# Low parts of weight tiles made by an accumulating DMA in a two-layer hybrid decoder kernel

## The chip, the cores and the metric

The kernel runs on one core of a Trainium2 chip. The metric is the device time of one execution in microseconds (us); lower is better. TensorE is called PE in the rows, its weight loads PEld, VectorE DVE, ScalarE ACT, GpSimd POOL, SyncE SP.

## What is computed

One inference step of a two-layer decoder trunk on 576 token rows (a prompt of 512 and 8 samples of 8), width 1024. All matrix products are in float32. The core of it is

```python
def swiglu(x, w_gate, w_up, w_down):
    return (jax.nn.silu(x @ w_gate) * (x @ w_up)) @ w_down
# each layer
x = x + 0.5 * swiglu(rms_norm(x, ffn1_norm), ffn1_w_gate, ffn1_w_up, ffn1_w_down)    # inner width 2816
proj = rms_norm(x, mix_norm) @ w_in                                                   # 1024 x 3092
...                                    # pool, GLA, HGRN2 and SSD mixers on parts of proj
x = x + jnp.concatenate([o_pool, o_gla, o_hgrn, o_ssm], axis=-1) @ w_out
x = x + 0.5 * swiglu(rms_norm(x, ffn2_norm), ffn2_w_gate, ffn2_w_up, ffn2_w_down)
```

with a last `rms_norm` after the two layers and new mixer states as further outputs.

## The kernel before

Every float32 product is made of three products of rounded operands. A weight tile w (128 rows, up to 1024 columns, that is up to eight 128x128 blocks) is split by `two_parts` into hi, w rounded to float32r, and lo = w - hi; activations are split alike by `split`. `gemm` then runs hi·hi (line 256), lo·hi (line 257) and hi·lo (line 258) for each block, in this order, so a tile's lo is wanted one matmul after its hi.

The host lays all weight tiles one after another into `wts` and lists them in `PLAN`, one entry (`what`, `at`, `n`, `tail`) per use, 491 in all, in the order in which PE takes them. `what` 0 is a tile used as it lies in memory. The feed-forward stages also multiply by a scheme with 7 products in place of 8: a round (`glu7`) takes four tiles b11, b21, b22, b12 from memory and makes seven operands of them in `ORDER` 1, 5, 6, 7, 3, 2, 4. Operand 1 is b11 itself, 2 is b12 and 4 is b22; 5, 6, 7 and 3 are sums and differences that VectorE makes in the `raws` buffers. There are 39 such rounds. A group of a feed-forward stage is up to three rounds and then eight tiles of the down projection (256 to 768 columns). Between the two feed-forward stages of a layer stands the mixer, whose 32 projection and output tiles without tail are all `what` 0, interleaved by `interleave` with the recurrences' small operations on every engine.

`weight()` hands the next tile to the matmuls and first prepares the tile three further on (`LOOKAHEAD` 3): `load` issues the DMA from `wts` on SP's queue into `raw` (2 buffers) or `raws` (4 buffers, shared with sums), and `two_parts` writes `whi` and `wlo` (4 buffers each). The buffers of the tile three ahead are those of the tile before the one just started, so a split can't begin before PE has read that one to its end. In the trace this shows as ACT waiting for line 258 ahead of line 195. The three last tiles of a stage that ends in a norm are marked `tail` and live in another pool. Within an engine instructions run in the order that the framework's scheduler gave them; nothing is reordered on the chip.

POOL has little to do: squares at the start, small copies in the mixers, and the shifted sums of the pooling mixer (`pool`, line 1197). It issues no DMA.

Of the kernel before, what the change touches and what calls it, by code (L numbers as in the profile page):

```python
# [5 lines left out]
F32 = mybir.dt.float32  # L6
F32R = mybir.dt.float32r
# [3 lines left out]
AF = mybir.ActivationFunctionType  # L11
ALU = mybir.AluOpType
# [95 lines left out]
class Trunk:  # L108
# [77 lines left out]
        return acts, self.sums(acts, self.first_norm(), range(KD))  # L186


    def two_parts(self, src, n, tail=False):
        nc = self.nc  # L190
        size = n if tail else 1024
        pool, th, tl, bufs = self.tail if tail else (self.wp, "whi", "wlo", (4, 4))
        hi = pool.tile([P, size], F32R, name="whi", tag=th, bufs=bufs[0])
        lo = pool.tile([P, size], F32R, name="wlo", tag=tl, bufs=bufs[1])
        nc.scalar.copy(hi[:, :n], src[:, :n])  # L195
        nc.vector.tensor_tensor(lo[:, :n], src[:, :n], hi[:, :n].bitcast(F32), ALU.subtract)  # L196
        return hi, lo

    def load(self, i, n, pool, tag, bufs):
# [4 lines left out]
    def prep(self, i):  # L204
        what, at, n, tail = self.plan[i]
        if what == 0:
            self.w[i] = self.two_parts(self.load(at, n, self.wp, "raw", 2), n, tail)
            return

        tt = self.nc.vector.tensor_tensor  # L210
        if what == 1:
            self.blocks = {11: self.load(at, n, self.sp, "raws", 4)}
            src = self.blocks[11]
        b = self.blocks
        if what == 5:
            b[21] = self.load(at + 1, n, self.sp, "raws", 4)
            b[22] = self.load(at + 2, n, self.wp, "raw", 2)
            b[12] = self.load(at + 3, n, self.wp, "raw", 2)
            src = b[0] = self.sp.tile([P, 1024], F32, name="raws", tag="raws", bufs=4)
            tt(src, b[21], b[22], ALU.add)  # L220
        elif what == 6:
            src = b[11]
            tt(b[21], b[11], b[21], ALU.subtract)
            tt(src, b[0], b[11], ALU.subtract)
        elif what == 7:
            src = b[21]
        elif what == 3:
            src = b[0]
            tt(src, b[12], b[11], ALU.subtract)
        elif what == 2:  # L230
            src = b[12]
        elif what == 4:
            src = b[22]
        self.w[i] = self.two_parts(src, n)

    def weight(self):
        i = self.wi
# [1294 lines left out]
```

## Time and profile before

| | |
|---|---|
| median of 3 runs | 2303.1 us (2296.84 to 2305.1) |
| the profiled execution | 2301.83 us, its span 2300.0 us |
| granted TensorE clock, mean | 0.989 of 2.4 GHz |
| busy: PE, DVE, ACT, POOL | 98%, 70%, 44%, 2% |
| read from memory | 180.36 MB, 81 GB/s over the span |
| share of the 16 DMA engines taken by SP's queue | 25.4% |

PE is busy in nearly all of the span, so a time saved elsewhere counts only where PE stands still or runs at the lower clock, and a time added counts where it makes PE wait. Matmul durations in the rows overlap: the starts of successive matmuls lie 0.13 us apart for 288 columns while each is listed with 0.29 us.

### The profile page before, as it was taken

The numbers are of one execution on the slowest core, as the hardware profiler recorded it, in microseconds if no ns is written. First come the engines' busy times: TensorE is split into PE (matmuls) and PEld (weight loads), VectorE is DVE, ScalarE is ACT, GpSimd is POOL, SyncE is SP. The second block draws the span as 40 slices with busy tenths as digits, with TensorE's granted clock in tenths as the row PEclk, the third lists the DMA queues.
The fourth block names the chain that finished last, engine by engine and source line by source line (L and its number), as shares of the span: only waits on it lengthen the run. The fifth ranks groups of instructions, "written<-read, shape, count | busy, mean of one in ns | idle before, by whom it ended". The sixth has DMA issues, their size and how long they took to land.

```text
span 2300.0 us, 40667 instructions
## 1 busy us (share of the span) xinstructions
PE 2253.3 (98%) x16721; PEld 2168.6 (94%) x16721; DVE 1619.4 (70%) x3049; ACT 1010.7 (44%) x1844; POOL 45.6 (2%) x94
## 2 busy tenths in 40 slices
PE   7999999999999999999999999999999999999997
PEld 6999999987978999999999999999889899999997
DVE  7775767777567876666697666767775688767575
ACT  3452534634424534344454443446344435435352
POOL 1000000000010000000000000000000100000000
PEclk9999999999989999999999999999999899999998
DMA  4232223211212133232313323232112131332322
GB/s 153 73 105 86 94 81 101 80 47 60 76 42 89 55 101 95 81 111 74 119 42 97 106 85 95 65 122 63 44 51 76 52 113 47 101 92 83 92 76 76
DMA packets 63146, 189.91 MB, mean 83 GB/s; under 512 B 7120, under 2 KB 13552, under 8 KB 62448
## 3 DMA queue, kind: packets, MB, share of 16 engines
q1 hardware_dynamic: 62816, 187.31, 25.4%
q8 instruction: 131, 2.15, 0.4%
q14 instruction: 55, 0.45, 0.1%
q10 hardware_dynamic: 144, 0.00, 0.0%
HBM read 180.36 MB, written 6.93 MB: 81 GB/s over the span
## 4 chain that ended last, share of the span: by engine, by line
PE 88%; DVE 7%; ACT 3%; DMA 1%; issue 1%; POOL 0%; ACTq 0%; DVEq 0%; SPq 0%
PE mm L258 21%; PE mm L256 21%; PE mm L257 20%; PE lv L256 3%; PE lv L258 3%; PE lv L257 3%; PE ms L258 2%; PE ms L257 2%; PE ms L256 2%; DVE wlo L196 1%; ACT whi L195 1%; PE lv L1182 1%; DMA raw<-wts 1%; DVE att L1187 1%; PE ms L1157 1%
## 5 line engine op out<-in xcount | busy, mean ns | idle before, releaser
L256 PE MATMUL mm<-h,whi 128*128 128x288 f32 (+2 forms) x1872 | 563.1, 302 | 10.0 <-ACT h L127 6.9
L258 PE MATMUL mm<-h,whi 128*128 128x288 f32 (+2 forms) x1872 | 558.6, 301 | 4.3 <-DVE h L128 4.2
L257 PE MATMUL mm<-h,wlo 128*128 128x288 f32 (+2 forms) x1872 | 560.0, 300 | 0.6 <-DVE wlo L196 0.6
L196 DVE TENSOR_TENSOR wlo<-raw,whi 128x1024 fp32r<-128x1024 f32 (+2 forms) x296 | 314.7, 1065 | 226.4 <-ACT whi L195 224.5
L256 PE MATMUL mm<-a,whi 128*128 128x256 f32 (+2 forms) x1408 | 414.5, 295 | 1.4 <-ACT a L278 1.3
L258 PE MATMUL mm<-a,whi 128*128 128x256 f32 (+2 forms) x1408 | 414.1, 295 | 0.6
L257 PE MATMUL mm<-a,wlo 128*128 128x256 f32 (+2 forms) x1408 | 414.3, 294 | 0.0
L256 PEld LDWEIGHTS mm<-h,whi 128*128 128x128 f32 x1872 | 357.6, 191 | 24.1 <-issue 10.6
L195 ACT CAST whi<-raw 128x1024 fp32r<-128x1024 f32 (+2 forms) x296 | 272.0, 921 | 242.7 <-PE mm L258 205.7
L258 PEld LDWEIGHTS mm<-h,whi 128*128 128x128 f32 x1872 | 356.6, 191 | 10.0 <-DVE h L128 5.5
L257 PEld LDWEIGHTS mm<-h,wlo 128*128 128x128 f32 x1872 | 357.5, 191 | 2.9 <-issue 1.6
L195 ACT CAST whi<-raws 128x1024 fp32r<-128x1024 f32 x195 | 204.7, 1050 | 178.2 <-PE mm L258 156.1
L196 DVE TENSOR_TENSOR wlo<-raws,whi 128x1024 fp32r<-128x1024 f32 x195 | 238.2, 1222 | 55.2 <-ACT whi L195 54.9
L258 PEld LDWEIGHTS mm<-a,whi 128*128 128x128 f32 x1408 | 263.8, 188 | 4.2 <-DVE a L279 4.1
L256 PEld LDWEIGHTS mm<-a,whi 128*128 128x128 f32 x1408 | 264.7, 188 | 2.1 <-ACT a L278 2.1
L257 PEld LDWEIGHTS mm<-a,wlo 128*128 128x128 f32 x1408 | 264.6, 188 | 0.0
L430 DVE SCALAR_TENSOR_TENSOR x<-mm,x 128x320 f32<-128x320 f32 (+2 forms) x256 | 116.6, 456 | 160.7 <-PE mm L258 160.2
L256 PE MATMUL mm<-more,whi 128*128 128x288 f32 x624 | 184.8, 296 | 0.4 <-ACT u L488 0.4
L257 PE MATMUL mm<-more,wlo 128*128 128x288 f32 x624 | 184.8, 296 | 0.3 <-DVE wlo L196 0.3
L258 PE MATMUL mm<-more,whi 128*128 128x288 f32 x624 | 185.0, 297 | 0.0
L256 PEld LDWEIGHTS mm<-more,whi 128*128 128x128 f32 x624 | 117.3, 188 | 1.5 <-ACT more L278 0.8
L257 PEld LDWEIGHTS mm<-more,wlo 128*128 128x128 f32 x624 | 117.5, 188 | 0.5 <-DVE wlo L196 0.5
(334 smaller groups left out, 3894.8 us busy)
## 6 DMA issues: line engine op xcount, KB each, us to landing
raw<-wts SPq DMA_DIRECT2D x156, 512.0 KB, 3.6
raw<-wts SPq DMA_DIRECT2D x106, 384.0 KB, 3.0
raws<-wts SPq DMA_DIRECT2D x78, 512.0 KB, 4.2
raw<-wts SPq DMA_DIRECT2D x32, 256.0 KB, 2.6
x<-x SPq DMA_DIRECT2D x4, 576.0 KB, 5.3
Ss<-sssm SPq DMA_DIRECT2D x2, 1024.0 KB, 6.0
nssm_s<-Ss SPq DMA_DIRECT2D x2, 1024.0 KB, 4.1
y<-x SPq DMA_DIRECT2D x4, 320.0 KB, 2.4
```

The source lines that it names most:

```text
L195: nc.scalar.copy(hi[:, :n], src[:, :n])
L196: nc.vector.tensor_tensor(lo[:, :n], src[:, :n], hi[:, :n].bitcast(F32), ALU.subtract)
L256: mm(ps[:, :n], wh, ah, start=(first and i == 0), stop=False)
L257: mm(ps[:, :n], wl, ah, start=False, stop=False)
L258: mm(ps[:, :n], wh, al, start=False, stop=(final and i == last))
L430: self.nc.vector.scalar_tensor_tensor(x, pd[:, :n], 0.5, x, ALU.mult, ALU.add)
L1157: nc.tensor.matmul(pu[d * s:d * s + d, :], kw[64:, si, d * s:d * s + d], vm[64:].rearrange("p b d -> p (b d)"), start=True, stop=True)
L1182: nc.tensor.matmul(lv[r, 0:4 * half], kc[:, 0], g2, start=True, stop=True)
L1187: nc.vector.copy_predicated(a2, mask.to_broadcast([n, 8, nb, w]), lv[r, 0:8 * half].rearrange("p (s b w) -> p s b w", s=8, w=w))
```

## The change

`two_parts` gets the tile's place in `wts` for 305 of the 491 operands: for `what` 0 without tail from the plan's thirteenth entry on, and for operands 1, 2 and 4 of the rounds. By width these are 181 of 1024 columns, 94 of 768, 28 of 512 and 2 of 256, together 139.5 MB; 117 of the 181 are those of the rounds. For them ScalarE writes -w, rounded to float32r, into `wlo`; POOL issues a DMA that reads the tile from memory once more and adds it onto `wlo`; then ScalarE writes `whi`. VectorE's subtraction falls away. The other 186 operands are made as before.

```diff
-    def two_parts(self, src, n, tail=False):
+    def two_parts(self, src, n, tail=False, at=None):
...
-        nc.scalar.copy(hi[:, :n], src[:, :n])
-        nc.vector.tensor_tensor(lo[:, :n], src[:, :n], hi[:, :n].bitcast(F32), ALU.subtract)
+        if at is None:
+            nc.scalar.copy(hi[:, :n], src[:, :n])
+            nc.vector.tensor_tensor(lo[:, :n], src[:, :n], hi[:, :n].bitcast(F32), ALU.subtract)
+        else:
+            nc.scalar.activation(lo[:, :n], src[:, :n], AF.Copy, scale=-1.0)
+            nc.gpsimd.dma_start(lo[:, :n], self.I["wts"][at, :, :n].bitcast(F32R), accum_op=ALU.add)
+            nc.scalar.copy(hi[:, :n], src[:, :n])
         return hi, lo
...
         if what == 0:
-            self.w[i] = self.two_parts(self.load(at, n, self.wp, "raw", 2), n, tail)
+            raw = self.load(at, n, self.wp, "raw", 2)
+            self.w[i] = self.two_parts(raw, n, tail, None if tail or i < 12 else at)
             return
...
-        self.w[i] = self.two_parts(src, n)
+        raw = {1: 0, 4: 2, 2: 3}.get(what)
+        self.w[i] = self.two_parts(src, n, False, None if raw is None else at + raw)
```

## Rows read from the trace of the kernel before

**Rows 1.** Page, part 1: the span, and busy us of each engine.
```profile
span 2300.0 us, 40667 instructions
PE 2253.3 (98%) x16721; PEld 2168.6 (94%) x16721; DVE 1619.4 (70%) x3049; ACT 1010.7 (44%) x1844; POOL 45.6 (2%) x94
```

**Rows 2.** Stretches: length, PE, PEld, DVE, ACT, POOL busy, clock, DMA share, GB/s.
```profile
0.00:100.00 100.00, 82.97 (x565) 80.44 (x566) 83.15 (x174) 40.61 (x82) 10.89 (x12) 0.95 0.37 123
900.00:1000.00 100.00, 99.95 (x754) 99.68 (x754) 66.48 (x95) 40.88 (x66) 0.00 (x0) 1.00 0.27 89
2200.00:2300.00 100.00, 87.57 (x652) 86.57 (x650) 64.93 (x128) 37.27 (x68) 0.00 (x0) 0.94 0.22 72
```

**Rows 3.** Stretches of 10 us in the first mixer, same columns.
```profile
650.00:660.00 10.00, 9.49 (x54) 9.12 (x55) 5.11 (x14) 1.06 (x4) 0.00 (x0) 0.67 0.00 1
670.00:680.00 10.00, 7.77 (x31) 6.25 (x29) 6.08 (x15) 1.18 (x3) 0.18 (x1) 0.70 0.13 39
```

**Rows 4.** Waits of PE: who for whom, us in total, times, longest.
```profile
PE ms L1252 <- DVE wide L1249: 4.2, 6, 1.4
PE lv L1182 <- DVE k L1061: 3.3, 7, 0.8
PE lv L874 <- DVE yc L912: 2.9, 2, 2.2
PE mm L257 <- DVE wlo L196: 0.9, 2, 0.6
```

**Rows 5.** Groups by shape, ACT's and DVE's: count, busy us, mean ns, idle before.
```profile
L195 ACT CAST whi<-raw 128x1024 fp32r<-128x1024 f32 x156 | 162.9, 1049 | 33.4 <-PE mm L258 16.0 <-DMA raw<-wts 12.7 <-PE mm L597 4.3
L195 ACT CAST whi<-raw 128x768 fp32r<-128x768 f32 x106 | 88.4, 834 | 158.3 <-PE mm L258 142.9 <-DMA raw<-wts 13.5
...
L196 DVE TENSOR_TENSOR wlo<-raw,whi 128x1024 fp32r<-128x1024 f32 x156 | 190.3, 1224 | 190.9 <-ACT whi L195 190.3
L196 DVE TENSOR_TENSOR wlo<-raw,whi 128x768 fp32r<-128x768 f32 x106 | 101.4, 957 | 29.6 <-ACT whi L195 28.4
```

**Rows 6.** Timeline of ACT in one round: start, us, line, operation.
```profile
953.01 1.05 ACT L195 CAST whi<-raw 128x1024 fp32r<-128x1024 f32 x1
...
956.21 1.05 ACT L195 CAST whi<-raw 128x1024 fp32r<-128x1024 f32 x1
...
959.27 1.04 ACT L195 CAST whi<-raws 128x1024 fp32r<-128x1024 f32 x1
```

**Rows 7.** Timeline of PE: a tile's last matmul, three tiles' first with wlo.
```profile
952.39 0.29 PE L258 MATMUL lv<-more,whi 128*128 128x288 f32 x1
...
962.25 0.29 PE L257 MATMUL ms<-h,wlo 128*128 128x288 f32 x1
...
965.41 0.30 PE L257 MATMUL mm<-h,wlo 128*128 128x288 f32 x1
...
968.61 0.29 PE L257 MATMUL mm<-h,wlo 128*128 128x288 f32 x1
```

**Rows 8.** Timeline of SP's queue: the loads issued beside these.
```profile
955.35 3.53 SPq L201 DMA_DIRECT2D raw<-wts  x2
958.93 0.43 SPq L201 DMA_DIRECT2D raws<-wts  x1
```

**Rows 9.** Page, part 6: DMA issues, count, KB each, median us to landing.
```profile
raw<-wts SPq DMA_DIRECT2D x156, 512.0 KB, 3.6
...
nssm_s<-Ss SPq DMA_DIRECT2D x2, 1024.0 KB, 4.1
...
nssm_p<-S SPq DMA_DIRECT2D x2, 128.0 KB, 1.7
```

**Rows 10.** DMA queue, 946 to 1013 us: packets, MB, share of 16 engines.
```profile
q1 hardware_dynamic: 1809, 6.03, 26.9%
```

**Rows 11.** Groups on POOL: count, busy us, mean ns, idle before.
```profile
L1197 POOL TENSOR_TENSOR pA<-pext 128x710 f32<-128x710 f32 x4 | 5.5, 1369 | 0.0
...
L718 POOL COPY nconv<-ext 128x3 f32<-128x3 f32 x12 | 3.3, 272 | 289.2 <-ACT ext L606 289.2
```

## The prediction

> **What bounds the kernel now.** I read the busy times first: PE is busy for 2253.3 of 2300.0 us, DVE for 1619.4, ACT for 1010.7 [rows 1]. Then the stretches of 100 us show where the missing 47 us of PE lie: 17.0 in the first stretch and 12.4 in the last, while a feed-forward stretch in the middle has 99.95 of 100 at full clock [rows 2]. The change leaves the first twelve plan entries and the last three tiles of each feed-forward stage alone, so the start and the end keep their gaps. What it can win lies in the mixers: there PE stands still for up to 2.2 us in 10, and the granted clock falls to 0.67 and 0.70 [rows 3]. The waits of PE say for whom: for VectorE's normalisation and recurrence steps (4.2, 3.3 and 2.9 us in total), and for a `wlo` written by VectorE hardly ever, 0.9 us in two waits [rows 4]. So VectorE's subtraction is not what PE waits for today. The kernel is bound by PE, and the question is whether the new way of making lo is ready when PE wants it.
>
> **What is removed.** Each wide subtraction takes 1.224 us, one of 768 columns 0.957 [rows 5]. 181 x 1.224 + 94 x 0.957 + (scaled by width from the 768 row) 28 x 0.64 + 2 x 0.32 = 330 us of DVE. In the feed-forward stages this is worth nothing: PE has no gap there [rows 2]. In the mixers (64 of the 305 operands) the subtractions stand between recurrence steps on DVE's queue. The three mixer waits of rows 4 sum to 10.4 us; I take about a third, 3 us, as gone. The rest stays, since those steps depend on each other and not only on the queue.
>
> **What ScalarE gets.** 305 extra passes, at the price of the cast beside them: 1.049 us wide, 0.834 at 768 [rows 5]; 181 x 1.049 + 94 x 0.834 + 28 x 0.56 + 2 x 0.28 = 285 us, which takes ACT from 1011 to about 1296 us of 2300. Behind them queue `whi`, 1.05 us later than now, and the evictions of PSUM banks, of which three are in rotation for most products. A `whi` has three tiles' time ahead of it, so I cost both at nothing; without that cover it would be up to 1 us per operand.
>
> **What the DMAs cost.** This is the term that decides. I take one round of the 7-product scheme, in a full-clock stretch. A tile is 24 matmuls long there, 3.2 us (962.25, 965.41, 968.61 in rows 7), so three tiles ahead is only 9.5 us. ACT begins operand 2's cast at 953.01, right after the buffer's last reader, which starts at 952.39 [rows 6, 7]. The negative pass in its place ends at 954.06, and PE wants lo at 962.25: 8.2 us. Operand 4: 957.26 to 965.41, 8.15 us. The next operand 1: 960.31 to 968.61, 8.3 us. The three accumulating operands are consecutive in `ORDER` from one round to the next (2, 4, 1), 3.2 us apart.
>
> No accumulating DMA and no DMA issued by POOL is in the trace. A plain load of 512 KB lands 3.6 us after its issue [rows 9]. Its bytes take 26.9% of 67 us = 18.0 us for 6.03 MB over three rounds, so 1.57 us per 512 KB with all 16 engines [rows 10]; 2.0 us is not data. An accumulate has to read the destination too. The nearest rows for reading SBUF are the stores: 1024 KB land in 4.1, 128 KB in 1.7, hence 1.4 us per further 512 KB [rows 9]. Bounds: 1.57 us of the engines, if reading the destination is free, and 6.4 us, if a whole load (3.6) and a whole 512 KB store (1.7 + 1.0 = 2.8, from the same slope) follow each other with nothing shared. I take 1.57 + 1.4 = 3.0 us, nearest to the load, because queued loads do overlap their fixed parts (three lie within 4 us in rows 8). For POOL's issue the nearest rows are SP's 0.43 us [rows 8] and a large POOL instruction, 1.37 us [rows 11]; I take 0.9, that is 0.5 above SP's.
>
> Alone, such a DMA takes 3.6 + 1.4 + 0.5 = 5.5 us and fits into 8.2. Three in a row with the loads of the next round do not quite. SP issues loads at 955.35, about 958.55 and 958.93 [rows 8]. They share the engines with the accumulates, and I count half of the last one as ahead of the third accumulate. From 954.1: 0.5 + 2.0 + 2.5 x 1.57 + 3 x 3.0 = 15.4, so the third lands at 969.5 where PE wants it at 968.61: 0.9 us late. PE has no slack to give this back, and the next triple meets the same queue 22 us later, with four operands in between that need no accumulate: 39 rounds x 0.9 = 35 us. At the lower bound the third lands 3.4 us early and nothing is lost; at the upper, 954.1 + 2.5 + 3.9 + 19.2 = 979.7, 11.1 us late, or 433 us over the rounds. The break-even is (968.61 - 954.1 - 2.5 - 3.9) / 3 = 2.7 us per 512 KB, close under my value.
>
> The Trainium skill, "Collectives: The Full Stack", section "The bandwidth ceiling: the fold count and why AG ≠ RS ≠ AR", says that a reducing transfer is slower than a copy not through the addition but through its two source reads, by a measured 1.93. By that ratio 512 KB would take an estimated 3.03 us of the engines, and the sum would be 1.0 us per round, 39 us. No run here shows it so far.
>
> **Other places.** In the down projections a 768-column tile takes 36 matmuls, about 4.7 us, and carries 384 KB: 0.75 x 3.0 + 0.75 x 1.57 = 3.4 us of the engines per 4.7, so it keeps up, as do the mixer projections (48 matmuls). POOL's queue: the new DMAs wait there for ACT's pass, and behind them stand the copies and shifted sums of the mixers; the reverse too, a DMA behind a copy that waits for ACT (289.2 us over 12 waits, rows 11, mostly because POOL has nothing earlier to do). The shifted sums end just before PE's 2.2 us gap [rows 3, 11]; one issue of 0.9 us in front of each of the four pools, 4 us in all, is its price, and I count it at 0, since the scheduler can put it on either side; it is kept for the range.
>
> **Sum.** 2301.8 (profiled execution) - 3 + 35 = 2334 us. The profiled execution lies 1.3 us under the median of the runs, so no correction is worth making.
>
> **The rivals.**
> - *Hidden.* An accumulate costs at most 2.7 us per 512 KB and POOL's issue is short, so every DMA lands before its tile. For it speaks that one alone fits with 2.7 us to spare; against it that 2.7 is under load plus store. Time: 2301.8 - 3 = about 2299, with POOL's 4 us at most 2303.
> - *Slow accumulate.* Adding and writing back run at less than the rate of the two reads, somewhere from 3.6 to 6.4 us per 512 KB. At 4.5: 954.1 + 2.5 + 3.9 + 13.5 = 974.0, 5.4 x 39 = 211, about 2510 us. For it: nothing in the trace bounds it below 6.4 except that copies pipeline.
> - *DMA engines as the bound.* The feed-forward stages take about 1600 us (2300 less two mixers of some 350). Their accumulates are worth 206 full tiles (117 in rounds, 12 other wide ones, 84 x 0.75 and 28 x 0.5 in down projections), their loads 264 (four for each round, all others one each), at 1.57 that is 415 us; the engines are full from (1600 - 415) / 206 = 5.75 us per 512 KB. At 7 us they alone need 1857 us there, and the kernel some 2560; with the late triples on top, 2600 or more.
> - *Faster.* This is the other side: the DMAs hidden, and VectorE's queue was what held the mixers. The mechanism is that a recurrence step no longer stands behind a 1.2 us subtraction, so PE neither waits nor drops to the lower clock. All waits of rows 4 (10.4 us) and, in each of the two mixers, about 7 us at the lower clock ([rows 3]: 3.3 + 3.0 in two stretches) sum to 24 us; it needs half of that to pass 0.5%: 2278 to 2290 us. Against it: DVE is busy for only 51 and 61% of those very stretches [rows 3].
>
> **How the numbers follow.** Forecast (2.7 to 3.6 us per 512 KB, which is 2300 to 2405, centre 2334): 0.34. Hidden: 0.31. Slow accumulate: 0.18. DMA-bound: 0.09. Faster: 0.08. The range of 2290 to 2510 leaves out most of "faster" below and the upper half of "slow" with the DMA-bound case above, together about 0.2. It takes in the forecast's own range. A measurement of this kernel can tell about 0.5% (11.5 us) from no change. Faster by more: 0.08. Within: the hidden case and the 0.03 of the forecast next to its lower end, 0.34. Slower by more: 0.58.
>
> **What would show it.** In the changed profile, PE should wait at line 257 for a DMA onto `wlo`, on operand 1 or 4 of the rounds most, 20 to 40 times, by about 1 us each; feed-forward stretches should fall from 99.95 to some 96 to 98. The issue row of `wlo<-wts` should read 5 to 6 us to landing, and more in the triples. DVE should fall to about 1290 us and ACT rise to about 1296. If the landing is under 5 us and there are no such waits, the accumulate is cheaper than load plus store and "hidden" is right. If the down projections wait too, it is above 4 us per 512 KB. The forecast would be wrong altogether if POOL's issue took several microseconds, or if the waits lay in the mixers behind POOL's copies.

## The result, and the profile after

The changed kernel takes 2404.32 us (median of 4 runs, 2388.56 to 2407.3) beside 2301.83 us of the kernel before (median of 4): 1.0437 times as long, 95% interval 1.0406 to 1.0468. The forecast had the direction, and its range holds the time, but of 102 us it foresaw 32.

The page of the changed kernel: the span, the busy times (as rows 1), the DMA queues, and the chain that ended last. Lines of the code lie 7 further down than before: 263 to 265 are the three matmuls of `gemm`, 199 ScalarE's negative pass, 200 POOL's DMA, 201 the cast behind it, 206 the load.

```profile
span 2401.9 us, 41456 instructions
PE 2287.6 (95%) x16721; PEld 2190.0 (91%) x16721; DVE 1303.4 (54%) x2744; ACT 1247.4 (52%) x2147; POOL 306.3 (13%) x399
q0 software_dynamic: 43920, 139.48, 32.9%
q1 hardware_dynamic: 62816, 187.31, 24.5%
PE 65%; DMA 20%; ACT 6%; DVE 6%; issue 3%; POOL 0%; ACTq 0%; DVEq 0%; SPq 0%; POOLq 0%
```

VectorE lost 316 us [rows 1] and nothing became faster. PE's idle time rose from 46.7 to 114.3 us, and its busy time by 34.3 for the same matmuls: the mean granted clock fell from 0.989 to 0.982. So some 68 of the 102 us are waiting. By the ratio of the two clocks the same matmuls would take about 16 us longer (an estimate: 2253.3 x 0.989 / 0.982); where the other 18 us of busy time come from was not taken apart. q0 is POOL's queue with the accumulates. In the chain that ended last DMAs now hold a fifth (before: 1%).

The issues of DMAs (rows 9 is the same view before), with KB each and the median us to landing:

```profile
wlo<-wts POOLq DMA_DIRECT2D x181, 512.0 KB, 6.8
raw<-wts SPq DMA_DIRECT2D x156, 512.0 KB, 6.0
raw<-wts SPq DMA_DIRECT2D x106, 384.0 KB, 5.5
```

The accumulate takes 6.8 us. But SP's own loads, which the change does not touch, went from 3.6 [rows 9] to 6.0 us, and those of 384 KB from 3.0 to 5.5. Who waits for that stands in the waits of PE (as rows 4), then of ACT, then of DVE: who for whom, us in total, times, longest.

```profile
PE ms L322 <- DVE sqs L312: 21.3, 5, 8.3
PE mm L263 <- ACT a L285: 16.7, 21, 2.5
PE mm L264 <- DMA wlo<-wts: 11.8, 21, 1.3
PE ms L264 <- DMA wlo<-wts: 11.2, 3, 4.0
PE mm L263 <- DVE x L437: 7.9, 6, 2.2
...
ACT wlo L199 <- DMA raw<-wts: 156.6, 77, 6.1
...
DVE raws L226 <- DMA raw<-wts: 119.5, 38, 6.5
```

PE waits for the accumulate itself (`wlo`) 23 us. It waits 46 us for squares of a norm (`sqs`), splits of activations (`a`) and residual sums (`x`), which have nothing to do with lo. What they share is the queue they stand in: ScalarE waits 156.6 us at its negative pass for a late `raw`, VectorE 119.5 us at the sums of the rounds. In the kernel before, ACT's cast waited 30.2 us for `raw` and DVE's sums 5.8; PE's waits for `sqs` were 2.9 us, for `a` 1.3, for `x` of line 430 (now 437) none.

SP issues a load of `one` early in each mixer and a store of `nssm_s` near its end. Before, then after (start, us, line, operation):

```profile
418.68 0.35 SPq L790 DMA_DIRECT2D one<-cst  x1
687.98 0.34 SPq L947 DMA_DIRECT2D nssm_s<-Ss  x1
1540.07 0.33 SPq L790 DMA_DIRECT2D one<-cst  x1
1817.04 0.34 SPq L947 DMA_DIRECT2D nssm_s<-Ss  x1
```
```profile
436.35 0.34 SPq L797 DMA_DIRECT2D one<-cst  x1
706.11 0.34 SPq L954 DMA_DIRECT2D nssm_s<-Ss  x1
1617.90 0.37 SPq L797 DMA_DIRECT2D one<-cst  x1
1894.37 0.34 SPq L954 DMA_DIRECT2D nssm_s<-Ss  x1
```

Between the marks of a mixer pass 269.3 and 277.0 us before, 269.8 and 276.5 after: no loss. All of it lies in the three stretches outside the marks, called the feed-forward stretches below: 17.7, 59.7 and 24.6 us. The second and the third begin with the end of a mixer, its output projection and the norm behind it.

Within them it is uneven. Stretches of 100 us of the changed kernel (columns as rows 2):

```profile
700.00:800.00 100.00, 90.92 (x621) 82.50 (x620) 59.83 (x160) 47.62 (x87) 7.78 (x9) 0.95 0.49 125
900.00:1000.00 100.00, 97.98 (x729) 96.74 (x728) 43.09 (x70) 52.71 (x80) 14.66 (x17) 1.00 0.69 158
```

900 to 1000 us, rounds and a down projection, falls from 99.95 [rows 2] to 97.98; 700 to 800, where a mixer's output ends in a norm and the next stage begins, reads 90.92 (before: 98.67). That place, in order of time (ACT, DVE, PE):

```profile
769.66 1.06 ACT L199 ACTIVATE wlo<-raw 128x1024 fp32r<-128x1024 f32 x1 [5.74 <-DMA raw<-wts]
...
771.57 0.44 ACT L311 ACTIVATE sq<-x 128x288 f32<-128x288 f32 x1
...
772.03 0.46 DVE L312 TENSOR_TENSOR sqs<-sqs,sq 128x288 f32<-128x288 f32 x1 [7.23 <-ACT sq L311]
...
778.24 1.23 DVE L226 TENSOR_TENSOR raws<-raws,raw 128x1024 f32<-128x1024 f32 x1 [2.94 <-DMA raw<-wts]
...
782.17 1.44 PE L322 MATMUL ms<-ones,sqs 128*128 128x1 f32 x6 [8.30 <-DVE sqs L312]
```

ScalarE waits 5.74 us for a late tile of the next stage, the square that the norm needs stands behind it, VectorE waits for the square and then for a late tile of its own, and PE stands still for 8.30 us. The same happens at 1970 us, behind the second mixer (8.34 us). Counted by `gemm`'s matmuls, the changed kernel falls back by 11.8 and 11.2 us within 200 matmuls at these two places, 23 of the 102 us.

### The profile page after: what moved, and what is told of

It is laid out like the page before. It is cut to its first block, busy times and chain, and to the rows that moved or that the text cites. A ratio compares the mean times of both kernels' runs of the same rounds, so it can differ in the third digit from the quotient of the medians.

```text
span 2401.9 us, 41456 instructions
## 1 busy us (share of the span) xinstructions
PE 2287.6 (95%) x16721; PEld 2190.0 (91%) x16721; DVE 1303.4 (54%) x2744; ACT 1247.4 (52%) x2147; POOL 306.3 (13%) x399
## 3 DMA queue, kind: packets, MB, share of 16 engines
q0 software_dynamic: 43920, 139.48, 32.9%
## 4 chain that ended last, share of the span: by engine, by line
PE 65%; DMA 20%; ACT 6%; DVE 6%; issue 3%; POOL 0%; ACTq 0%; DVEq 0%; SPq 0%; POOLq 0%
PE mm L263 16%; PE mm L264 16%; PE mm L265 15%; DMA raw<-wts 14%; DMA wlo<-wts 6%; PE lv L263 2%; PE lv L264 2%; PE lv L265 2%; ACT whi L201 2%; ACT wlo L199 2%; PE lv L1189 1%; DVE att L1194 1%; PE ms L1164 1%; PE lv L1191 1%; PE mm L604 1%
## 5 line engine op out<-in xcount | busy, mean ns | idle before, releaser
L200 POOL DMA_DIRECT2D wlo<-wts x305 | 263.5, 864 | 1956.8 <-ACT wlo L199 1049.6
L199 ACT ACTIVATE wlo<-raw 128x1024 fp32r<-128x1024 f32 (+2 forms) x266 | 248.1, 934 | 404.3 <-PE mm L264 198.2
L263 PE MATMUL mm<-a,whi 128*128 128x256 f32 (+2 forms) x1408 | 420.5, 299 | 24.8 <-ACT a L285 16.7
L265 PE MATMUL mm<-a,whi 128*128 128x256 f32 (+2 forms) x1408 | 418.9, 298 | 0.0
L263 PEld LDWEIGHTS mm<-a,whi 128*128 128x128 f32 x1408 | 267.1, 190 | 30.8 <-ACT a L285 21.3
L265 PEld LDWEIGHTS mm<-a,whi 128*128 128x128 f32 x1408 | 267.1, 190 | 4.2 <-DVE a L286 4.2
L201 ACT CAST whi<-raw 128x1024 fp32r<-128x1024 f32 (+2 forms) x266 | 243.1, 914 | 0.0
L197 DVE TENSOR_TENSOR wlo<-raws,whi 128x1024 fp32r<-128x1024 f32 x156 | 190.2, 1219 | 60.9 <-ACT whi L196 60.9
L196 ACT CAST whi<-raws 128x1024 fp32r<-128x1024 f32 x156 | 163.7, 1049 | 110.4 <-PE mm L265 78.1
L530 DVE TENSOR_TENSOR p<-mm,p 128x288 f32<-128x288 f32 x78 | 35.5, 455 | 196.8 <-PE mm L265 196.8
```

The lines of the kernel that those rows point to most:

```text
L199: nc.scalar.activation(lo[:, :n], src[:, :n], AF.Copy, scale=-1.0)
L200: nc.gpsimd.dma_start(lo[:, :n], self.I["wts"][at, :, :n].bitcast(F32R), accum_op=ALU.add)
L263: mm(ps[:, :n], wh, ah, start=(first and i == 0), stop=False)
L265: mm(ps[:, :n], wh, al, start=False, stop=(final and i == last))
L530: tt(s[j], ps, s[j], ALU.add)
```

## The experiments

Theories at the start. **A**: the accumulate itself lands too late (the forecast's). **L**: the accumulates slow SP's loads, and ScalarE and VectorE, which work in order, stand waiting for `raw` while what PE needs queues behind. **S**: ScalarE's extra passes and the new order cost the time. The stage lengths of all runs come from the marks above, in profiled executions; FF are the three feed-forward stretches. Only the two kernels, e18, e14, e15 and e16 were executed more than once. Single executions of a kernel differ by several us, those of the changed kernel by up to 19 (2388.56 to 2407.3), so a difference of 3 us means nothing here.

| kernel (accumulates) | us | FF 1, 2, 3 | FF sum | two mixers |
|---|---|---|---|---|
| before (0) | 2301.8 | 418.7, 852.1, 483.0 | 1753.7 | 546.3 |
| the change (305) | 2403.7 | 436.4, 911.8, 507.5 | 1855.7 | 546.2 |
| e1_no_dma | 2301.5 | 416.9, 852.6, 483.3 | 1752.8 | 547.0 |
| e2_plain_pool (305 plain) | 2316.6 | 418.9, 860.6, 489.9 | 1769.5 | 545.4 |
| e9_half (305 halves) | 2319.9 | 417.7, 864.7, 488.0 | 1770.3 | 547.9 |
| e5_what0 (188) | 2373.1 | 429.3, 892.7, 504.8 | 1826.8 | 544.5 |
| e6_rounds (117) | 2343.9 | 422.9, 874.0, 492.9 | 1789.8 | 552.3 |
| e4c_small (305) | 2396.2 | 431.9, 898.5, 505.3 | 1835.7 | 558.8 |
| *three buffers for raw:* | | | | |
| e18, kernel before (0) | 2292.9 | 419.4, 851.0, 482.6 | 1753.0 | 538.1 |
| e4_raw3 (305) | 2343.8 | 422.3, 868.1, 491.5 | 1781.9 | 560.1 |
| e12_raw3_what0 (188) | 2318.8 | 420.8, 852.7, 485.2 | 1758.7 | 558.4 |
| e13_raw3_rounds (117) | 2320.2 | 419.2, 865.0, 491.3 | 1775.6 | 542.8 |
| e14, later rounds (108) | 2305.6 | 422.8, 855.8, 485.5 | 1764.1 | 539.7 |
| e15, first rounds (9) | 2306.6 | 418.1, 862.1, 486.5 | 1766.6 | 538.2 |
| e16, no first, no mixer (232) | 2314.8 | 421.4, 863.3, 488.7 | 1773.4 | 539.7 |

### The DMA left out

```diff
-            nc.gpsimd.dma_start(lo[:, :n], self.I["wts"][at, :, :n].bitcast(F32R), accum_op=ALU.add)
```

> Leaves out the 305 accumulating DMAs, so lo is only the negative high part; ScalarE's extra pass, VectorE's relief and the order of the queues stay. Theory L (SP's loads land late because the accumulates share the DMA engines, and ScalarE and VectorE stand in order behind them) and theory A (PE waits for the accumulate itself) both expect about 2300 us, 2295 to 2310, with raw loads back at 3.6 us to landing. Theory S (the extra ScalarE pass and the changed order delay evictions and splits by themselves) expects 2350 us or more.

Measured 2301.54 us beside 2298.9 of the kernel before. `lo` is then only the negative high part. Its busy times:

```profile
PE 2249.1 (98%) x16721; PEld 2168.7 (94%) x16721; DVE 1311.9 (57%) x2744; ACT 1261.7 (55%) x2147; POOL 42.6 (2%) x94
```

All the passes and no DMA cost 2.6 us, within the noise: S falls. VectorE's sums wait 37.5 us for `raw` here and it costs nothing, so such a wait alone is no loss. It is also the price of an accumulate that costs nothing, and it says what VectorE's 308 us are worth. Nothing: the mixers take 547.0 us with them gone and 546.3 with them there. The rival "faster" falls with it.

### The second read without the addition

```diff
-            nc.gpsimd.dma_start(lo[:, :n], ..., accum_op=ALU.add)
+            nc.gpsimd.dma_start(lo[:, :n], ...)
```

> The 305 DMAs of POOL overwrite wlo instead of adding onto it, so lo is the whole weight; the bytes read from memory, the issues and all waits stay, only the reading of the destination goes. If the engines' time per 512 KB falls from 2.97 to about 1.6 us, theory L expects the loss of 102 us to shrink by about half or more (2310 to 2360 us) and raw loads to land at 4 to 5 us. Theory A expects 2300 to 2315, as such a DMA then lands 1.4 us sooner and reaches every tile in time. If the time stays at 2400, the price is in the issue or in the second read of memory and not in the adding.

Measured 2316.64 us. POOL's queue, and the issues:

```profile
q0 software_dynamic: 43920, 139.48, 21.0%
wlo<-wts POOLq DMA_DIRECT2D x181, 512.0 KB, 3.9
raw<-wts SPq DMA_DIRECT2D x156, 512.0 KB, 4.4
```

The same bytes in the same places, but 21.0% of 2314.9 us over 266 full tiles' bytes (139.48 MB) is 1.83 us of the engines per 512 KB; for the accumulate it is 32.9% of 2401.9, 2.97 us. The loads land at 4.4 and the loss is 15 to 18 us in place of 102. ACT's waits for `raw` at its negative pass fall to 45.5 us. The loss falls with the time that the DMAs hold the engines, far more than in proportion. Since the DMA itself also lands sooner (3.9 for 6.8 us), this run alone does not tell L from A.

### Half of each accumulate

```diff
-            nc.gpsimd.dma_start(lo[:, :n], self.I["wts"][at, :, :n].bitcast(F32R), accum_op=ALU.add)
+            m = n // 2
+            nc.gpsimd.dma_start(lo[:, :m], self.I["wts"][at, :, :m].bitcast(F32R), accum_op=ALU.add)
```

> The changed kernel with the accumulating DMA on the first half of the columns only; the other half of lo stays the negative high part. Bytes of the accumulates halve, their number and order stay. Both theories expect the engines' time per DMA to halve to about 1.5 us for a wide tile, under the break-even of 2.7 us of the prediction, and so 2300 to 2315 us. Were the loss a matter of the count of DMAs (issue, fixed latency), half or more of the 102 us would stay, 2350 or above.

Measured 2319.93 us beside 2299.43, q0 at 18.9%, loads of 512 KB landing at 4.4, PE's waits for `wlo` 5.4 us. The first half of the bytes costs 20 us, some 5 more than either theory expected, the second half 84: the loss grows much faster than the bytes, as L and A both have it.

### One part of the change alone

```diff
# e5_what0: accumulates for tiles of kind 0 alone
-        raw = {1: 0, 4: 2, 2: 3}.get(what)
+        raw = None
# e6_rounds: accumulates for operands 1, 2 and 4 of the rounds alone
-            ... None if tail or i < 12 else at)
+            ... None)
```

> Accumulates only for the 188 tiles taken as they lie (down projections, mixers, first pairs); the rounds' 117 operands are split by VectorE as before. The prediction put the whole loss into the rounds, so by it this run has about 2300 us. Theory L puts it where loads of raw tiles and accumulates follow one another tile by tile, in the change from rounds to down projections and at the norms; it expects 2340 to 2390 us.

> Accumulates only for the 117 operands of the rounds. The prediction expects 2325 to 2340 us from waits of PE for wlo (the 23 us of waits seen in the changed kernel). Theory L expects a similar or smaller part here, 2310 to 2340, since SP's loads are further apart in the rounds. The two parts together need not add up to 102 us; if this part alone gives 2380 or more, the rounds are the place after all.

Measured 2373.11 and 2343.92 us. The kind-0 tiles alone lose 73 us in the feed-forward stretches, with PE's waits

```profile
PE mm L263 <- ACT a L285: 22.6, 15, 3.5
PE ms L322 <- DVE sqs L312: 21.8, 6, 8.3
PE mm L263 <- DVE x L437: 10.6, 9, 1.9
```

and none for an accumulate onto `wlo`. So for most of the change A is wrong: these accumulates are in time, and PE stands still all the same, for operations that wait behind a late `raw` on ACT (81.9 us) or DVE (53.5 us).

How that looks in the changed kernel, in the down projection after a round: ACT's timeline (start, us, operation, in brackets its idle time and what ended it), then the DMA queues in 930 to 956 us (packets, MB, share).

```profile
935.28 0.85 ACT L199 ACTIVATE wlo<-raw 128x768 fp32r<-128x768 f32 x1 [1.97 <-DMA raw<-wts]
...
939.66 0.85 ACT L199 ACTIVATE wlo<-raw 128x768 fp32r<-128x768 f32 x1 [2.14 <-DMA raw<-wts]
...
943.81 0.85 ACT L199 ACTIVATE wlo<-raw 128x768 fp32r<-128x768 f32 x1 [1.90 <-DMA raw<-wts]
...
945.28 0.43 ACT L285 CAST a<-p 128x288 fp32r<-128x288 f32 x1
...
q0 software_dynamic: 892, 2.71, 56.0%
q1 hardware_dynamic: 1007, 2.75, 43.1%
```

The two queues fill the 16 engines for 26 us, where the 100 us from 900 read 0.69 in the mean. The load is 2 us late each time, and the cast of `a`, on which the next matmul depends, stands behind the pass that waits. PE waits for it, and reads 4.23 of 5 us busy between 945 and 950.

### A third buffer for raw

```diff
-            raw = self.load(at, n, self.wp, "raw", 2)
+            raw = self.load(at, n, self.wp, "raw", 3)
... the same for b22 and b12; sq, rs_v and the mixers' ext go from 2 buffers to 1 to make room
```

e4c_small has the smaller buffers alone, as a control.

> Control for the next run: the changed kernel with one buffer instead of two for the squares of the norms, for one small row of the inverse root and for the mixers' ext rows, which makes room for a third raw buffer but doesn't use it. Both theories expect it within 10 us of the changed kernel, 2395 to 2415; a larger time is the price of the room.

> The same with three raw buffers in place of two, so SP's loads may be issued a tile earlier; the accumulates and their bytes are as in the changed kernel. Theory L (late loads hold ScalarE and VectorE) expects 40 to 70 us less than the control, with ScalarE's waits for raw (156.6 us in the changed kernel) falling under 50. Theory A (late accumulates) expects no gain, within 10 us of the control, or a loss, since loads then run into the accumulates.

Measured 2396.24 and 2343.8 us. ACT's and DVE's waits for `raw`, of the control and then, with its DMA rows, of the kernel with three buffers:

```profile
ACT wlo L199 <- DMA raw<-wts: 142.6, 71, 6.3
DVE raws L226 <- DMA raw<-wts: 112.8, 38, 5.1
```
```profile
ACT wlo L199 <- DMA raw<-wts: 13.6, 8, 3.1
DVE raws L226 <- DMA raw<-wts: 52.0, 14, 6.1
q0 software_dynamic: 43920, 139.48, 33.3%
raw<-wts SPq DMA_DIRECT2D x156, 512.0 KB, 6.4
```

The DMAs are as slow as before, even a little slower; the loads are only issued earlier. That removes most of ScalarE's wait and 52 us, and PE's waits for `sqs` fall from 19.1 to 7.5 us, for `a` from 10.4 to 0.4. In the feed-forward stretches the loss is 102 us in the change, 82 in the control and 29 with three buffers: 53 us are the third buffer's own. The 20 us between the change and the control come with the smaller buffers or lie in the spread of single executions; that was not told apart. So L is shown for the larger part. The two mixers take 558.8 us in the control already, so their extra 12 to 22 us come from the smaller buffers together with the accumulates (which of the three buffers was not tried); the change itself does not have them.

### The same two parts with three buffers

e12 and e13 are e5 and e6 with three buffers for `raw`, e18 is the kernel before with them, and e11_before_raw3 a single execution of the same kernel as e18.

> Control: the kernel before with the smaller buffers and three raw buffers, no accumulate. Both theories expect 2295 to 2310; if it is faster than that, the third buffer is a gain of its own, and its 52 us in the changed kernel can't all be put down to loads that the accumulates delay.

> Three raw buffers, accumulates only for the 188 tiles taken as they lie. Theory L says that their loss (72 us with two raw buffers) is late raw loads, so with the third buffer 2300 to 2320 us remain. If 2340 or more remain, the third buffer helped the rounds and not these tiles.

> Three raw buffers, accumulates only for the rounds' 117 operands. The prediction's term (three consecutive operands late by about 1 us in 39 rounds, 35 us) doesn't depend on raw loads being early: by it about 2330 to 2345 us remain, as with two buffers (2344). If it falls to 2300 to 2315, late raw loads were the loss in the rounds too.

Measured 2296.19, 2318.82 and 2320.2 us. In the feed-forward stretches kind 0 falls from +73 to +6 us, the rounds from +36 to +23; together 29, as in e4_raw3. The rounds' 2320.2 us lie between the two ranges: the third buffer helped them, but not to 2315. Of the 26 us that e12 lies above e18, 20 are the mixers with the smaller buffers.

### Where the rounds' rest lies

The trace of e13 showed three single waits of 2.5 to 4.0 us for `wlo`, each in the round that follows a norm. **T** is the forecast's theory (a little in each of 39 rounds), **F** says that only those three rounds lose. Both kernels accumulate nothing for kind 0 and have three buffers, as e13. A round is marked `first` when the plan's entry before it is a wide tile of kind 0.

```diff
         if what == 1:
+            self.first = self.plan[i - 1][:3:2] == (0, 1024)
...
# e14: the later rounds
-        ... None if raw is None else at + raw)
+        ... None if raw is None or self.first else at + raw)
# e15: the first rounds
-        ... None if raw is None else at + raw)
+        ... at + raw if raw is not None and self.first else None)
```

> The kernel before with three buffers for raw (one for sq, rs_v and the mixers' ext, to make room), no accumulate: the base for the runs beside it. Its one look gave 2296.2 beside 2301.7. If the third buffer itself is a gain: 2294 to 2298, 4 to 7 us under the kernel before. If that was noise: within 2 us of it.

> Three raw buffers; accumulates only for operands 1, 2 and 4 of the 36 rounds that do not follow a norm (108 operands), none for tiles of kind 0. Theory T (the prediction's: three consecutive accumulates are late in each round, some 0.6 us): 2296 + 36 x 0.6 = about 2316 to 2320. Theory F (only the rounds right after a norm lose, since ScalarE's passes are late there and 6 to 8 us follow until the landing, where VectorE needed 1.2): 2296 to 2302, with PE's waits for a DMA onto wlo under 5 us in total.

> Three raw buffers; accumulates only for operands 1, 2 and 4 of the three rounds that follow a norm: 9 operands of 491. Theory T: 2296 + 3 x 0.6 = 2297 to 2299. Theory F: three PE waits of 2.5 to 4 us for a DMA onto wlo and a lower clock behind each, together 12 to 20 us: 2308 to 2316.

Medians 2294.79, 2304.53 and 2308.75 us. Nine operands cost 14.0 us and the other 108 cost 9.7; the sum, 23.7, is what the rounds cost together (25). F holds for more than half. The later rounds' 9.7 us lie between what T (some 20) and F (at most 6) expected: 0.27 us a round in the mean, with PE's waits for `wlo` 5.3 us in ten waits altogether. What happens in such a place: the timeline of e15's ACT, POOL and PE with its row of PE's waits, then e18's ACT, DVE and PE at the same round.

```profile
796.67 2.00 ACT L199 ACTIVATE wlo<-raw 128x1024 fp32r<-128x1024 f32 x2
...
798.04 1.79 POOL L200 DMA_DIRECT2D wlo<-wts  x2 [19.77 <-ACT wlo L199]
...
804.77 0.59 PE L265 MATMUL ms<-h,wlo 128*128 128x288 f32 x1 [3.87 <-DMA wlo<-wts]
...
PE ms L265 <- DMA wlo<-wts: 10.2, 3, 3.9
```
```profile
797.74 2.00 ACT L195 CAST whi<-raw 128x1024 fp32r<-128x1024 f32 x2
...
799.60 2.35 DVE L196 TENSOR_TENSOR wlo<-raw,whi 128x1024 fp32r<-128x1024 f32 x2
...
802.91 0.30 PE L257 MATMUL ms<-h,wlo 128*128 128x288 f32 x1
```

After a norm VectorE and ScalarE are busy with the splits of the activations, and the operand's pass comes late in both kernels. From ACT's start to the lo of operand 2 VectorE needs 3.1 us (797.74 to about 800.8) and PE comes 2.1 us later. The accumulate needs 8.1 (796.67 to 804.77) and PE waits 3.87 of them. The three waits add up to 10.2 of the 14 us. The granted clock of the ten us from 800 reads 0.83 there (1.00 in e18): part of the matmuls behind the pause run at the lower clock, which fits the other 3.8 us but was not measured apart.

### All but the first rounds and the mixers

```diff
-            ... None if tail or i < 12 else at)
+            ... None if tail or i < 12 or 103 <= i < 138 or 350 <= i < 385 else at)
```

with e14's edit and three buffers: 232 operands.

> Three raw buffers; accumulates as in the change, but for the three rounds that follow a norm and for the projections of the two mixers. Theory F, with the other loss in the mixers (stage marks of the run with kind 0 alone: +11 and +6 us in the mixers, +5 in all the rest): 2298 to 2306. If the share of the DMA engines makes operands late all over the feed-forward stages, third buffer or not: 2325 to 2340.

Median 2320.24 us (2314.82 to 2322.93): 25.5 above e18, where F with nothing else expected at most 11; it lies between that and the 2325 of the other reading. In the profiled execution, the lowest of the four, the mixers are free of loss (539.7 us) and the stretches lose 20 us, 9 more than e14 without the kind-0 tiles. PE's waits for `sqs` rise from 2.9 to 7.8 us, and waits for `x` of 6.6 us appear. So even with three buffers the down projections are not quite free.

### The traffic alone

e8b_traffic keeps VectorE's subtraction and accumulates onto a buffer that nobody reads.

```diff
         nc.vector.tensor_tensor(lo[:, :n], src[:, :n], hi[:, :n].bitcast(F32), ALU.subtract)
+        if at is not None:
+            nc.gpsimd.dma_start(spare[:, :n], self.I["wts"][at, :, :n], accum_op=ALU.add)
```

> Traffic beside the kernel before, without the POOL copy that made the previous run hold whi: VectorE makes lo as before, and the 305 accumulating DMAs go onto a spare tile, each waiting for the one before it and for nothing else. No engine reads or waits for them. Theory L expects raw loads to land later than 3.6 us, ScalarE to wait for them, and 2320 to 2370 us. Theory A expects 2300 to 2312. If it is 2395 again, the loss needs only the traffic.

Measured 2699.89 us, and not what it was made for. All accumulates go to one buffer, so they follow each other, and POOL waits for each: 1457.4 us. PE's longest wait, VectorE's and POOL's:

```profile
PE mm L264 <- ACT q L990: 239.9, 2, 239.4
DVE rows L812 <- POOL cv L796: 239.5, 1, 239.5
POOL spare L202 <- DMA spare<-wts: 1457.4, 299, 9.1
```

POOL's small operations of the first mixer (`cv`) stood behind the backlog, and the mixer stood still: 631.5 us between its marks. Before it, from 100 to 400 us, at 0.71 to 0.77 of the engines, PE is busy for 96.68, 99.95 and 97.32 us per 100, where the kernel before has 99.95 in each. From 100 us to the mixer's mark ScalarE's casts wait 25.5 us for `raw` (before: 5.2), and up to it PE waits 5.5 us for `a` and 3.5 for `x` (before: none). No operand here depends on an accumulate, so this is what L says of the traffic; as a total the run decides nothing. An earlier form, e8_traffic, in which POOL also copied a column of `hi`, made ScalarE wait 273.4 us for that copy and says as little (2396.37 us).

> The kernel before with hi and lo made by ScalarE and VectorE as before, plus the 305 accumulating DMAs onto a spare tile that no engine reads, each released when its tile's hi is written (and with the smaller buffers of the control). Nothing waits for an accumulate but the next one. Theory L expects 30 to 80 us above before, 2335 to 2385, with raw loads landing later than 3.6 us and ScalarE waiting for them. Theory A expects 2300 to 2315.

## Why the prediction was right and wrong

**What bounds the kernel, and VectorE.** Right that PE did not wait for the subtraction. The 3 us counted for the mixers were nothing (e1).

**ScalarE at no cost.** Right in e1. The busy time is 1247 instead of 1296 us; passes back to back overlap by 0.1 us (the one of 0.85 us at 935.28 is followed at 936.03), which for 305 of them explains some 30 of the 49 (an estimate). But the cover that was named, three tiles of lead, assumed that `raw` is there. With late loads the passes hold up the queue.

**The accumulate's price.** Estimated 3.0 us of the engines, measured 2.97; POOL's issue 0.9, measured 0.864 in the mean and at most 1.011, so nothing held an issue up. The 5.5 us forecast from ACT's pass to the landing of one alone were about right (5.5 from POOL's issue, one after the other, in e8b_traffic); in the changed kernel it was 6.8. The ratio to a plain load, 2.97 to 1.57 [rows 10], is 1.89; the Trainium skill's 1.93 ("Collectives: The Full Stack", "The bandwidth ceiling: the fold count and why AG ≠ RS ≠ AR") agrees with this trace. But that section speaks of rings between cores, and against POOL's own overwriting DMA (1.83, e2) the ratio is 1.62, so the match hangs on what one divides by. A slip in the bounds, 1.7 + 1.0 = 2.8 where it is 2.7, moves only the upper one, from 6.4 to 6.3. The price was right, and yet the sum was not.

**The rounds, 0.9 us x 39 = 35.** With two buffers e6 lost 36 us in the feed-forward stretches. That is the forecast's size by luck: 13 of them are gone with three buffers, and what remains is 14 us in three rounds after a norm and some 10 in the other 36, a third of the 0.9 us each. The waits for `wlo` in the changed kernel are 18 in rounds (the sign was 20 to 40), 11.2 of their 19.5 us in three of them, and 6 in down projections. The sum was made for a round in the steady state and had no place where ScalarE's pass comes late.

**"It keeps up, as do the mixer projections."** The step that failed, for the down projections; between the mixers' marks it held. It compared the mean load of the engines, 3.4 us in 4.7, and found room. The wide tiles of kind 0 with which a feed-forward stage begins had no term in the sum at all, and at two of the three places where one begins 23 us were lost. In the trace the queues fill the engines for 26 us together behind a round's three accumulates, loads land 2.4 us later in the median of all, and with two `raw` buffers they were not issued early enough to bear that. ACT and DVE wait, in order, and PE waits for their other work: 73 us (e5) where 0 stood. The forecast followed the added DMA to its own reader and did not ask what it does to the DMAs that were there. Its sign for this, that the down projections would wait only above 4 us per 512 KB, was wrong: they waited at 2.97. Its sign that the stretches would fall to 96 to 98 came true (97.98), but not for its reason.

**Where the 102 us went.** All into the feed-forward stretches. By the runs with three buffers, 53 of them, measured against the control, are late loads on two buffers, and up to 73 if the 20 between the change and the control are counted with them. Of the rest 14 are the rounds after a norm, some 10 the other rounds, and 6 to 9 the remaining tiles; the parts overlap by a few us. What costs the 10 us in the other rounds beyond the waits for `wlo` was not tried.

**The rivals.** "Hidden" needed 2.7 us per 512 KB and missed it by 0.3. "Slow accumulate" and "DMA engines as bound" had the price wrong, and "Faster" fell with e1. None of the four was what happened. That the range holds 2404 us is luck: within the forecast such a time stood for 3.6 us per 512 KB with all of the loss in the rounds, and above 2405 for a dearer accumulate.

**A version that beats both.** The kernel before with three buffers for `raw` and the smaller others takes 2294.79 us beside 2300.42: 0.9981, interval 0.9972 to 0.9990. The gain lies in the mixers (538.1 for 546.3 us), the feed-forward stretches are as before, so it is not shown that the third `raw` buffer makes it. With accumulates no version here was faster than that; with the DMA at no cost at all the change gains nothing.

## What to carry to other kernels

Before moving work onto DMAs, price what the added traffic does to the loads that are already there, and ask how many buffers of lead those loads have: an in-order engine that waits for a late tile holds up everything queued behind it, so the loss shows as waits for operations that have nothing to do with the edit. A mean share of the engines under one is no proof of room: here 0.69 over 100 us held 26 us at 0.99. And first measure what the relief itself is worth, by leaving the added operation out: here it was nothing.

## What had not been expected of the hardware

The second read of the memory is not the dear part of the accumulate: it takes 2.97 us of the engines per 512 KB and 6.8 us to landing, where the same read as an overwrite took 1.83 and 3.9. How much of the difference is the adding and how much the reading of the destination, no run here tells. And a DMA that POOL issues waits in POOL's own queue: a backlog of them held the mixer's small operations for 239 us (e8b_traffic). PE's pauses may cost beyond their length: ten us with a pause of 3.87 us and the matmuls behind it had a granted clock of 0.83 in the mean (e15), against 1.00 in the same ten us of e18.
